# A decoder trunk with 32 experts: expert weights in 2048-column pieces, both turns in one place, and a written order of ScalarE and VectorE at the end

## The chip, the cores and the metric

The kernel runs on one core of one Trainium2 chip. The metric is device microseconds (us) from the first to the last instruction of one execution with what lies around it; lower is better. TensorE is PE here (its weight loads are PEld), VectorE is DVE, ScalarE is ACT, GpSimd is POOL, SyncE is SP. All data are fp32.

## The reference

One decoder layer over 1024 tokens of width 1024, then a final RMSNorm. The first half of the layer mixes tokens (an SSD group, a forgetting-attention group, a convolution group, one output projection); the second is a mixture of 32 gated-MLP experts, two for each token:

```
x = x + g_m * hybrid_mixer(rms_norm(x, norm_mix_g) * (1.0 + sc_m) + sh_m, ...)
h = rms_norm(x, norm_ffn_g) * (1.0 + sc_f) + sh_f
# per token: one group of 8 experts, in it the two best, with weights sw
hid = silu(xb @ w_gate[e]) * (xb @ w_up[e])      # 1024 -> 512
y   = hid @ w_down[e]                            # 512 -> 1024
out = zeros.at[stok].add(ys[dest] * sw)          # the two shares of a token
x = x + g_f * out
return rms_norm(x, final_norm_g)
```

## The kernel before

**An fp32 product.** TensorE multiplies a rounded form of fp32, so each operand is cut in two: `hi` is a cast of it (made by ACT), `lo` is what the cast left (a subtraction by DVE). A product is three matmuls: hi with `xh`, hi with `xl`, lo with `xh`, where `xh` and `xl` are the two parts of the tokens. So every weight that arrives from DRAM passes once through ACT (`phi`) and once through DVE (`plo`) before PE may use it.

**The experts.** From about 645 us to 1237 us the program goes through the experts in order. An expert has 6 MB of weights: gate (G), up (U) and down (D), each 2 tiles of 2048 columns ("halves"), loaded by SP into a ring of 18 such halves (`NHALF`, `load_half`) that runs ahead of the use. `piece` (L1325 to L1329) takes 1024 columns: one cast and one subtraction, with three buffers for each result. 6 matmuls use a piece, so an expert is 12 pieces and 72 matmuls of 512 columns. The loop body of expert e runs G(e), U(e), then D(e-1), so the hidden activations `hid` have time to be made. Two "turns" (groups of 128x128 transposes on PE with a split by ACT and DVE behind them) feed this: `xpose(e+1)` turns the 128 gathered tokens of the next expert (8 transposes `ps_xg`, then `xh`, `xl`), and `turn_hidden` turns `hid` (4 transposes `ps_ht`, then `hh`, `hl`). In before, `turn_hidden(e-1)` is called ahead of the second piece of G(e) (`before_down`), `xpose` ahead of the second piece of D(e-1). When D(e-1) is done, DVE scales it by the router's weight and the gate `gf` (two `early` operations, L1374), and POOL adds it into the result in DRAM with an indirect DMA, called the scatter here (L1378); POOL also gathers the next tokens (L1308).

**Order of the work.** Each engine runs its own list in order. A scheduler makes the lists from the order of the code and from its estimates; instructions that are pinned (`pin`) keep the order in which the code writes them.

**Ahead of the experts.** `row_spread(gf, ...)` (L1282) spreads a row over all partitions by 8 pairs of small matmuls and two copies. In the mixer, the q and k tiles (`qk_tile`, matmuls `ps_pr`) run on PE while DVE does the convolution (`cy`); one transpose, `ps_nc` (L487), takes a running sum `ncu` (L481) that DVE makes.

**The end.** When the last but one share has been scattered, SP loads the eight blocks of the result (`x_d`); blocks 0 to 5 are normed and written at once, without the share of expert 31 (ACT: `Square` with a sum; DVE and POOL: the factor; DVE: the product). The rows among them that have such a share are gathered into `xr` (the tile `xg`) by POOL. Blocks 6 and 7 get the share of expert 31 by matmuls with a matrix of places (`ps_ad`), `xr` gets it by an addition; `xr` is normed too, and POOL scatters it over the output last (L1485).

## Time and profile before

| | |
|---|---|
| three runs, median | 1276.93 us (1276.75 to 1277.41) |
| the profiled execution | 1275.77 us, of which the span of its instructions 1273.9 us |
| PE busy | 1186.6 us, 93% of the span |
| DVE, ACT, POOL busy | 980.5, 736.4, 268.2 us |
| mean granted TensorE clock | 0.972 |
| one steady expert | 18.46 us (scatters at 904.48 and 922.97 us, for one pair) |

Times inside the trace count from the first instruction. "Busy" is an engine's time in instructions; where rows carry a bracket, it is how long the engine stood idle ahead of that row, and what ended the wait. Rows that the profile puts together as "x3" overlap: their time is from the start of the first to the end of the last.

### The profile page before, as it was taken

To read this page: it belongs to the slowest core of one execution; us is meant where nothing else is said; L and a number is where in the kernel's file an instruction comes from. 1 tells how busy PE (TensorE), PEld (TensorE's weight loads), DVE (VectorE), ACT (ScalarE), POOL (GpSimd) and SP (SyncE) were. 2 spreads that over 40 slices of the span, in tenths; PEclk is the share of its full clock that TensorE was granted. 3 is DMA by queue.
4 is the path that set the end of the run, shared out by engine and by line. 5 is a ranking of instruction groups with operands and counts; after the bars stand their busy time and mean duration, and the time that the engine had idled before them with its cause. 6 is when DMAs were issued, how large, how long until landed. Compare 5 with 4: busy or idle time off the path is not lost. (4 is left out here: it accounts for less than half of the span.)

```text
span 1273.9 us, 17238 instructions
## 1 busy us (share of the span) xinstructions
PE 1186.6 (93%) x6079; PEld 928.3 (73%) x6079; DVE 980.5 (77%) x1395; ACT 736.4 (58%) x1145; POOL 268.2 (21%) x200
## 2 busy tenths in 40 slices
PE   6999989999999779999779999999999999999993
PEld 4676757868678568778568877777877787787772
DVE  4789992145265676575559999999999999999985
ACT  4323322343354656563258877777877787777763
POOL 3110313100100353432111221122112212211112
PEclk9999999999999989999879999999999999999997
DMA  9316667633201553734889999999999999999726
GB/s 361 140 42 220 210 196 224 160 108 89 78 17 59 148 155 100 262 98 183 304 305 343 361 356 372 366 354 367 369 359 372 356 358 387 363 381 366 236 53 257
DMA packets 93339, 313.21 MB, mean 246 GB/s; under 512 B 23894, under 2 KB 34310, under 8 KB 70976
## 3 DMA queue, kind: packets, MB, share of 16 engines
q1 hardware_dynamic: 60750, 256.25, 54.8%
q10 hardware_dynamic: 14242, 32.51, 7.4%
q0 software_dynamic: 18256, 23.30, 7.2%
q8 instruction: 49, 0.80, 0.3%
q14 instruction: 42, 0.34, 0.1%
HBM read 289.22 MB, written 39.88 MB: 258 GB/s over the span
## 5 line engine op out<-in xcount | busy, mean ns | idle before, releaser
L1342 PE MATMUL ps_gu<-plo,xh 128*128 128x512 f32 x512 | 209.1, 408 | 9.1 <-DVE plo L1328 9.0
L1340 PE MATMUL ps_gu<-phi,xh 128*128 128x512 f32 x512 | 203.3, 397 | 1.4 <-ACT xh L127 1.4
L1328 DVE TENSOR_TENSOR plo<-wx,phi 128x1024 fp32r<-128x1024 f32 x166 | 198.1, 1220 | 7.8 <-ACT phi L1328 5.5
L1328 ACT CAST phi<-wx 128x1024 fp32r<-128x1024 f32 x166 | 173.1, 1054 | 50.7 <-PE ps_gu L1341 40.8
L1341 PE MATMUL ps_gu<-phi,xl 128*128 128x512 f32 x512 | 200.8, 392 | 0.0
L1378 POOL DMA_INDIRECT x_d<-early,toki x31 | 74.9, 2416 | 400.7 <-DVE early L1374 386.0
L1328 ACT CAST phi<-w 128x1024 fp32r<-128x1024 f32 x110 | 115.3, 1050 | 60.4 <-PE ps_gu L1341 53.1
L1328 DVE TENSOR_TENSOR plo<-w,phi 128x1024 fp32r<-128x1024 f32 x110 | 130.7, 1220 | 7.2 <-ACT phi L1328 6.3
L1342 PEld LDWEIGHTS ps_gu<-plo,xh 128*128 128x128 f32 x512 | 96.3, 188 | 40.2 <-DVE plo L1328 20.8
L1340 PEld LDWEIGHTS ps_gu<-phi,xh 128*128 128x128 f32 x512 | 96.5, 189 | 20.2 <-ACT xh L127 1.8
L1341 PEld LDWEIGHTS ps_gu<-phi,xl 128*128 128x128 f32 x512 | 96.5, 188 | 19.6
L1368 PE MATMUL ps_d<-phi,hh 128*128 128x512 f32 x256 | 100.4, 393 | 0.7 <-ACT hh L127 0.7
L1369 PE MATMUL ps_d<-phi,hl 128*128 128x512 f32 x256 | 100.5, 393 | 0.0
L1370 PE MATMUL ps_d<-plo,hh 128*128 128x512 f32 x256 | 96.4, 393 | 0.0
L182 PE MATMUL ps_pr<-h_hi,whi 128*128 128x512 f32 x224 | 91.5, 409 | 0.0
L184 PE MATMUL ps_pr<-h_hi,wlo 128*128 128x512 f32 x224 | 88.8, 396 | 1.3 <-POOL wlo L128 1.3
L183 PE MATMUL ps_pr<-h_lo,whi 128*128 128x512 f32 x224 | 89.2, 398 | 0.0
L225 DVE SCALAR_TENSOR_TENSOR cy<-u_t,cmw,cy 128x1024 f32<-128x1024 f32 x60 | 86.4, 1440 | 2.3 <-ACT cy L222 1.4
L128 POOL TENSOR_TENSOR wlo<-wraw,whi 128x1024 fp32r<-128x1024 f32 x14 | 40.0, 2866 | 161.1 <-ACT whi L127 142.9
L1328 DVE TENSOR_TENSOR plo<-cy,phi 128x1024 fp32r<-128x1024 f32 x44 | 53.8, 1222 | 6.0 <-ACT phi L1328 5.2
L994 PE MATMUL ps_wo<-wo_hi,yh 128*128 128x512 f32 x128 | 55.1, 431 | 2.1 <-ACT yh L127 2.1
L1368 PEld LDWEIGHTS ps_d<-phi,hh 128*128 128x128 f32 x256 | 48.3, 189 | 10.9 <-ACT hh L127 0.9
(405 smaller groups left out, 2570.9 us busy)
## 6 DMA issues: line engine op xcount, KB each, us to landing
w<-in_w_gu_dram SPq DMA_DIRECT2D x54, 1024.0 KB
wx<-in_w_gu_dram SPq DMA_DIRECT2D x50, 1024.0 KB
...
```

What stands on the lines that cost most here:

```text
L182: PE.matmul(ps, hi[:, kt, :], h_hi[hf][:, kt, :], start=(kt == 0), stop=False)
L183: PE.matmul(ps, hi[:, kt, :], h_lo[hf][:, kt, :], start=False, stop=False)
L184: PE.matmul(ps, lo[:, kt, :], h_hi[hf][:, kt, :], start=False, stop=(kt == KT - 1))
L225: yield lambda t=t, k=k: V.scalar_tensor_tensor(cy[:, :, t], v128(u_t[:, t, k:k + T]), cmw[:, t, k:k + 1], cy[:, :, t], op0=ALU.mult, op1= ...
L1328: last[:] = [S.copy(hi, raw).ins, V.tensor_tensor(lo, raw, hi.bitcast(F32), op=ALU.subtract).ins]
L1340: PE.matmul(ps, xh[:, kt], hi[:, ks], start=(kt == 0), stop=False)
L1341: PE.matmul(ps, xl[:, kt], hi[:, ks], start=False, stop=False)
L1342: PE.matmul(ps, xh[:, kt], lo[:, ks], start=False, stop=(kt == KT - 1))
L1368: PE.matmul(pd[n], hh[:, f], hi[:, ns], start=(f == 0), stop=False)
L1369: PE.matmul(pd[n], hl[:, f], hi[:, ns], start=False, stop=False)
L1370: PE.matmul(pd[n], hh[:, f], lo[:, ns], start=False, stop=(f == 3))
L1378: G.indirect_dma_start(x1_d[:, :], bass.IndirectOffsetOnAxis(ap=toki[:, e:e + 1], axis=0), yo[:, :], None, bounds_check=T - 1, oob_is_err= ...
```

## The change

1. **Pieces of 2048 columns.** `piece` becomes `pieces`: one cast and one subtraction of 2048 columns for a half, two buffers for each result in place of three. PE's order in a piece is 8 matmuls with hi, then 4 with lo, pinned. Halves that lie in two tiles (`wy`) and the last down projection stay in two parts of 1024.
2. **Turns together.** `xpose(e+1)` and `turn_hidden(e)` are both called in the middle of D(e-1). `hh` and `hl` lie in one tile `hx`.
3. **Room.** The ring has 17 halves; `w2` goes.
4. **The last experts.** D(30) is placed ahead of G(31), and its share has a buffer of its own (`free[1]`), not `early`. Its weights are loaded ahead of those of G(31).
5. **Rows.** `row_spread(gf)` moves from before expert 0 into the middle of the body of expert 1, `row_spread(fng)` into that of expert 30.
6. **`ps_nc`** moves behind the second q and k tile (t == 1) and is pinned.
7. **The end.** The order of ACT and DVE is written out: squares of the six blocks on ACT, four products on DVE ahead of the scaling of the last share, the addition to `xr` on DVE (in before POOL), the addition of EPS on POOL, output in halves of a block.

```diff
-NHALF = 18
+NHALF = 17
...
-DC, NC_ = 2, 15
+DC, NC_ = 2, 14
...
-        if t == 0:
+        if t == 1:
             pc = bank("ps_nc")
-            PE.transpose(pc[:32, 0:P], ncu.rearrange("p h b -> p (h b)"), ident)
+            pin(PE.transpose(pc[:32, 0:P], ncu.rearrange("p h b -> p (h b)"), ident))
...
-        order += [(e, 0), (e, 1), (e - 1, 2)] if e < NE - 1 else [(e, 0), (e - 1, 2), (e, 1)]
+        order += [(e, 0), (e, 1), (e - 1, 2)] if e < NE - 1 else [(e - 1, 2), (e, 0), (e, 1)]
...
-            room(ew.tile([P, 2048], F32, name="w2"))
...
-    row_spread(gf, sl[0:8, :])
...
+        def pieces(e, m, s):
+            a, b, both = wts[e, m][s]
+            hi = ex.tile([P, 2048], F32R, tag="phi", name="phi", bufs=2)
+            lo = ex.tile([P, 2048], F32R, tag="plo", name="plo", bufs=2)
+            if both is None or (e, m) == (NE - 1, 2):
+                parts = ((a, slice(0, 1024)), (b, slice(1024, 2048)))
+            else:
+                parts = ((both, slice(0, 2048)),)
+            for raw, cs in parts:
+                last[:] = [S.copy(hi[:, cs], raw).ins, V.tensor_tensor(lo[:, cs], raw, hi[:, cs].bitcast(F32), op=ALU.subtract).ins]
+            return [(hi[:, cs], lo[:, cs], (cs.stop - cs.start) // 512) for _, cs in parts]
...
+                for hi, lo, n in pieces(e, m, s):
+                    for k in range(n):
+                        ks = slice(512 * k, 512 * (k + 1))
+                        pin(PE.matmul(ps, xh[:, k0 + k], hi[:, ks], start=(k0 + k == 0), stop=False))
+                        pin(PE.matmul(ps, xl[:, k0 + k], hi[:, ks], start=False, stop=False))
+                    for k in range(n):
+                        ks = slice(512 * k, 512 * (k + 1))
+                        pin(PE.matmul(ps, xh[:, k0 + k], lo[:, ks], start=False, stop=(k0 + k == KT - 1)))
+                    k0 += n
...
+            def middle():
+                next_tokens(e + 1)
+                turns()
+                if e == 1:
+                    row_spread(gf, sl[0:8, :])
+                if e == NE - 2:
+                    row_spread(fng, early[0:8, D:D + P])
...
+            if e == NE - 1:
                 down(e - 1, *hts[e - 1])
                 load_next()
-                hid = hidden(pg, gate_or_up(e, 1, xh, xl))
+            pg = gate_or_up(e, 0, xh, xl, turns if e == 1 else None)
+            load_next()
+            hid = hidden(pg, gate_or_up(e, 1, xh, xl))
+            load_next()
+            if e == 0:
+                next_tokens(1)
+            elif e < NE - 1:
+                down(e - 1, *hts[e - 1], middle)
                 load_next()
...
+        sqs = [square(xbs[b]) for b in range(FB)]
+        for b in range(4):
+            finish(b, sqs[b])
         for n in range(2):
             ns = slice(512 * n, 512 * (n + 1))
-            split(yh[:, ns], yl[:, ns], yo_l[:, ns])
+            pin(V.scalar_tensor_tensor(yo_l[:, ns], pd[n], wtab[:, NE - 1:NE], gf[:, ns], op0=ALU.mult, op1=ALU.mult))
...
+            pin(S.copy(yh[:, ns], yo_l[:, ns]))
+            pin(V.tensor_tensor(yl[:, ns], yo_l[:, ns], yh[:, ns].bitcast(F32), op=ALU.subtract))
+        pin(V.tensor_tensor(xr, xr, yo_l, op=ALU.add))
+        sx = square(xr)
+        for b in range(4, FB):
+            finish(b, sqs[b])
```

**VectorE, one steady expert.** Before, from the `hid` of one expert to the first subtractions of the next body (`plo` are the subtractions, `xl` and `hl` the splits of the two turns):

```order
L1348 TENSOR_TENSOR hid<-hid,ps_gu 128x512
L1328 TENSOR_TENSOR plo<-wx,phi 128x1024
L128 TENSOR_TENSOR xl<-ps_xg,xh 128x512 x2
L1328 TENSOR_TENSOR plo<-wx,phi 128x1024 x2
L1374 SCALAR_TENSOR_TENSOR early<-ps_d_6666,wtab,gf 128x512
L1374 SCALAR_TENSOR_TENSOR early<-ps_d_6667,wtab,gf 128x512
L1328 TENSOR_TENSOR plo<-wx,phi 128x1024
L128 TENSOR_TENSOR hl<-ps_ht,hh 128x512
L1328 TENSOR_TENSOR plo<-wy,phi 128x1024 x2
L1328 TENSOR_TENSOR plo<-w_4443,phi 128x1024 x4
L1328 TENSOR_TENSOR plo<-xq_3956,phi 128x1024 x2
```

In the changed kernel, the same stretch of the same expert:

```order
L1331 TENSOR_TENSOR plo<-wx,phi 128x2048 x2
L126 TENSOR_TENSOR xl<-ps_xg,xh 128x512 x2
L126 TENSOR_TENSOR hx<-ps_ht,hx 128x512
L1391 SCALAR_TENSOR_TENSOR early<-ps_d_7683,wtab,gf 128x512
L1391 SCALAR_TENSOR_TENSOR early<-ps_d_7684,wtab,gf 128x512
L1331 TENSOR_TENSOR plo<-wx,phi 128x2048
L1331 TENSOR_TENSOR plo<-wy,phi 128x1024 x2
L1331 TENSOR_TENSOR plo<-w_4443,phi 128x2048 x2
L1355 TENSOR_TENSOR hid<-hid,ps_gu 128x512
L1331 TENSOR_TENSOR plo<-xq_3956,phi 128x2048
```

Between the subtraction of the first gate half and that of the second there now stand five operations in a row (`xl` twice, `hx`, `early` twice); before, they were spread between five subtractions.

**TensorE around `ps_nc`.** Before, it stands within the matmuls of a q or k tile, ahead of `ps_arr` and `ps_a` (products for the modulation):

```order
L182 MATMUL ps_pr_1408<-h_hi_106,whi 128x512
L183 MATMUL ps_pr_1408<-h_lo_108,whi 128x512
L487 MATMUL ps_nc<-ident,ncu 32x128
L423 MATMUL ps_arr<-aacc,ind_r 128x512 x2
L415 MATMUL ps_a_1367<-at,cond_119 32x512 x8
L184 MATMUL ps_pr_1408<-h_hi_106,wlo 128x512
L182 MATMUL ps_pr_1408<-h_hi_106,whi 128x512
```

Now `ps_arr` and a first group of `ps_a` stand alone there:

```order
L181 MATMUL ps_pr_1314<-h_lo_109,whi 128x512
L182 MATMUL ps_pr_1314<-h_hi_107,wlo 128x512
L421 MATMUL ps_arr<-aacc,ind_r 128x512 x2
L413 MATMUL ps_a_1362<-at,cond_119 32x512 x8
L180 MATMUL ps_pr_1403<-h_hi_106,whi 128x512
L181 MATMUL ps_pr_1403<-h_lo_108,whi 128x512
```

and `ps_nc` comes after 48 further matmuls `ps_pr`, behind the second tile:

```order
L181 MATMUL ps_pr_1428<-h_lo_109,whi 128x512
L182 MATMUL ps_pr_1428<-h_hi_107,wlo 128x512
L485 MATMUL ps_nc<-ident,ncu 32x128
L421 MATMUL ps_arr<-aacc,ind_r 128x512 x2
L413 MATMUL ps_a_1481<-at,cond_119 32x512 x8
L180 MATMUL ps_pr_1522<-h_hi_106,whi 128x512
```

**VectorE at the end.** Before, from the split of the last `hid` on (L1293 is the addition of EPS, L1296 the product of a block, L1374 the scaling of the last share, `yo_l` its split):

```order
L128 TENSOR_TENSOR hl<-ps_ht,hh 128x512
L1328 TENSOR_TENSOR plo<-wx,phi 128x1024
L1293 TENSOR_SCALAR s_11117<-s_11117 128x1
L1296 SCALAR_TENSOR_TENSOR wx<-wx,s_11117 128x1024
L1374 SCALAR_TENSOR_TENSOR wx<-ps_d_11073,wtab,gf 128x512
L1374 SCALAR_TENSOR_TENSOR wx<-ps_d_11074,wtab,gf 128x512
L1293 TENSOR_SCALAR s_11123<-s_11123 128x1
L1293 TENSOR_SCALAR s_11129<-s_11129 128x1
L1296 SCALAR_TENSOR_TENSOR wx<-wx,s_11123 128x1024
L1296 SCALAR_TENSOR_TENSOR wy<-wy,s_11129,wx 128x1024
L1293 TENSOR_SCALAR s_11135<-s_11135 128x1
L128 TENSOR_TENSOR yo_l<-wx,yo_h 128x512
```

Now (L1486 is the product of a block, L1494 the scaling, L1501 the addition to `xr`):

```order
L126 TENSOR_TENSOR hx<-ps_ht,hx 128x512
L1486 SCALAR_TENSOR_TENSOR wx<-wx,s_10363,wy 128x1024
L1486 SCALAR_TENSOR_TENSOR wx<-wx,s_10367,wy 128x1024
L1486 SCALAR_TENSOR_TENSOR wx<-wx,s_10371,wy 128x1024
L1486 SCALAR_TENSOR_TENSOR wx<-wx,s_10375,wy 128x1024
L1494 SCALAR_TENSOR_TENSOR cy<-ps_d_10325,wtab,gf 128x512
L1494 SCALAR_TENSOR_TENSOR cy<-ps_d_10326,wtab,gf 128x512
L1500 TENSOR_TENSOR yo_l<-cy,yo_h 128x512 x2
L1501 TENSOR_TENSOR xg<-xg,cy 128x1024
L1486 SCALAR_TENSOR_TENSOR wx<-wx,s_10379,wy 128x1024
L1486 SCALAR_TENSOR_TENSOR wx<-wx,s_10383,wy 128x1024
L1522 SCALAR_TENSOR_TENSOR s_10412<-s_10412 128x1
```

The additions of EPS are gone from DVE, four products come first, and the scaling, the split and the addition follow one another.

## Rows read from the trace of the kernel before

**Rows 1.** The page: GB/s moved by DMA in 40 equal slices of the span.
```profile
GB/s 361 140 42 220 210 196 224 160 108 89 78 17 59 148 155 100 262 98 183 304 305 343 361 356 372 366 354 367 369 359 372 356 358 387 363 381 366 236 53 257
```

**Rows 2.** Windows: busy us of PE, PEld, DVE, ACT, POOL; clock, DMA share, GB/s.
```profile
300.00:400.00 100.00, 99.82 (x563) 72.86 (x562) 48.61 (x122) 42.81 (x81) 8.95 (x7) 1.00 0.18 56
...
800.00:900.00 100.00, 98.32 (x456) 79.67 (x455) 96.17 (x98) 78.13 (x90) 17.29 (x10) 1.00 0.99 363
```

**Rows 3.** Waits from 700 to 1200: total us, times, longest us.
```profile
PEld ps_gu L1342 <- DVE plo L1328: 18.7, 25, 0.8
...
SPq L1198 <- DVE plo L1328: 208.1, 107, 4.4
```

**Rows 4.** Timeline of PE in one steady expert: start us, us.
```profile
913.20 0.39 PE L1340 MATMUL ps_gu<-phi,xh 128*128 128x512 f32 x1
...
914.56 0.39 PE L1340 MATMUL ps_gu<-phi,xh 128*128 128x512 f32 x1
...
923.02 1.03 PE L1318 MATMUL ps_xg<-ident,xg 128*128 128x128 f32 x8
...
925.86 0.50 PE L1342 MATMUL ps_gu<-plo,xh 128*128 128x512 f32 x1 [0.33 <-DVE plo L1328]
```

**Rows 5.** Timeline of DVE in the same expert.
```profile
917.81 1.28 DVE L128 TENSOR_TENSOR xl<-ps_xg,xh 128x512 fp32r<-128x512 f32 x2
...
919.01 2.35 DVE L1328 TENSOR_TENSOR plo<-wx,phi 128x1024 fp32r<-128x1024 f32 x2
...
921.28 1.41 DVE L1374 SCALAR_TENSOR_TENSOR early<-ps_d,wtab,gf 128x512 f32<-128x512 f32 x2
```

**Rows 6.** Timeline of ACT in the same expert.
```profile
916.17 1.06 ACT L127 CAST xh<-ps_xg 128x512 fp32r<-128x512 f32 x2
...
917.12 2.01 ACT L1328 CAST phi<-wx 128x1024 fp32r<-128x1024 f32 x2
```

**Rows 7.** Timeline of POOL: the first and the thirtieth scatter, of 30.
```profile
684.70 3.47 POOL L1378 DMA_INDIRECT x_d<-early,toki  x1 [4.21 <-DVE early L1374]
...
1218.51 2.28 POOL L1378 DMA_INDIRECT x_d<-early,toki  x1 [16.15 <-DVE early L1374]
```

**Rows 8.** Timeline of PE around the transpose ps_nc, in the front.
```profile
169.72 0.40 PE L183 MATMUL ps_pr<-h_lo,whi 128*128 128x512 f32 x1
...
175.38 0.37 PE L487 MATMUL ps_nc<-ident,ncu 128*32 128x128 f32 x1 [5.27 <-DVE ncu L481]
...
176.54 2.94 PE L415 MATMUL ps_a<-at,cond 128*32 128x512 f32 x16
```

**Rows 9.** Timeline of DVE there.
```profile
175.06 0.18 DVE L481 TENSOR_SCALAR ncu<-early 128x32 f32<-128x32 f32 x1
```

**Rows 10.** Timeline of PE ahead of expert 0.
```profile
643.86 3.75 PE L1282 MATMUL ps_row<-sl,ident 8*128 8x128 f32 x16 [5.48 <-DMA sl<-g_rows]
...
647.54 1.97 PE L1318 MATMUL ps_xg<-ident,xg 128*128 128x128 f32 x8
```

**Rows 11.** Timeline of DVE there: the largest of seven overflow operations.
```profile
648.17 0.39 DVE L1394 TENSOR_TENSOR c<-cnt,j 128x224 f32<-128x224 f32 x1
```

**Rows 12.** Timelines of POOL, SP, ACT and DVE at the end.
```profile
1231.90 2.29 POOL L1378 DMA_INDIRECT x_d<-early,toki  x1 [11.11 <-DVE early L1374]
...
1238.75 0.81 SPq L1446 DMA_DIRECT2D wx<-x_d  x2
...
1251.93 1.06 ACT L1292 ACTIVATE wx<-w 128x1024 f32<-128x1024 f32 x1 [2.01 <-DMA w<-x_d]
...
1246.44 1.43 DVE L1374 SCALAR_TENSOR_TENSOR wx<-ps_d,wtab,gf 128x512 f32<-128x512 f32 x2 [0.17 <-PE ps_d L1370]
...
1256.60 3.36 DVE L1296 SCALAR_TENSOR_TENSOR w<-w,s,wx 128x1024 f32<-128x1024 f32 x1 [0.66 <-POOL s L1294]
...
1264.20 1.28 DVE L1296 SCALAR_TENSOR_TENSOR xg<-xg,s,wx 128x1024 f32<-128x1024 f32 x1 [0.73 <-POOL s L1294]
...
1265.77 1.06 POOL L1485 DMA_INDIRECT out_dram<-xg,toki  x1 [1.61 <-DVEq L1489]
```

More of the change, by code (lines that the diff above doesn't have):

```diff
@@ L49 @@
 ZW = 2
-QT = 1
 DEPTH = 5
@@ L1194, in load_half @@
             src = (w_gu[e, m_] if m_ < 2 else w_dn[e]).rearrange("p a c -> p (a c)")[:, 2048 * (i % 2):2048 * (i % 2 + 1)]
-            w, both = halves[i % NHALF][0:2], halves[i % NHALF][2]
-            pieces = ((both, src),) if both is not None and i < 6 * NE - 6 else zip(w, (src[:, 0:1024], src[:, 1024:2048]))
+            w = halves[i % NHALF]
+            both = w[2]
+            pieces = ((both, src),) if both is not None and i < 6 * NE - 6 else zip(w[0:2], (src[:, 0:1024], src[:, 1024:2048]))
             for dst, sc_ in pieces:
@@ L1361, in down @@
             pd = [bank("ps_d0", "pj"), bank("ps_d1", "pj")]
-            for f in range(4):
-                if f == QD and then:
+            f0 = 0
+            for s in range(2):
+                if s and then:
                     then()
-                hi, lo = piece(e, 2, f)
-                for n in range(2):
-                    ns = slice(512 * n, 512 * (n + 1))
-                    PE.matmul(pd[n], hh[:, f], hi[:, ns], start=(f == 0), stop=False)
-                    PE.matmul(pd[n], hl[:, f], hi[:, ns], start=False, stop=False)
-                    PE.matmul(pd[n], hh[:, f], lo[:, ns], start=False, stop=(f == 3))
-            yo = yo_l if e == NE - 1 else early[:, 0:D]
+                for hi, lo, w in pieces(e, 2, s):
+                    fn = [(f0 + i // 2, i % 2, slice(512 * i, 512 * (i + 1))) for i in range(w)]
+                    for f, n, ns in fn:
+                        pin(PE.matmul(pd[n], hh[:, f], hi[:, ns], start=(f == 0), stop=False))
+                        pin(PE.matmul(pd[n], hl[:, f], hi[:, ns], start=False, stop=False))
+                    for f, n, ns in fn:
+                        pin(PE.matmul(pd[n], hh[:, f], lo[:, ns], start=False, stop=(f == 3)))
+                    f0 += w // 2
+            if e == NE - 1:
+                return pd
+            yo = free[1] if e == NE - 2 else early[:, 0:D]
             for n in range(2):
@@ L1436, in mixer_moe @@
                 overflow()
-            if e == NE - 2:
-                free = [h for k in (8, 7, 6) for w in wts[order[3 * NE - k]] for h in w]
         yo_l, junk, tok = free[0:3]
@@ L1453, in mixer_moe, with square, finish @@
         V.tensor_scalar(place, tok[:, 0:T - nf], tok_l[:, 0:1], None, op0=ALU.is_equal)
[L1454 to L1459 removed]
+        pd = down(NE - 1, *turn_hidden(NE - 1, hid))
+        def square(src):
+            s3 = late.tile([P, 2], F32, tag="s3e", name="s3", bufs=7)
+            pin(S.activation(junk, src, AF.Square, scale=1.0 / 32, accum_out=s3[:, 0:1]))
+            G.tensor_scalar(s3[:, 0:1], s3[:, 0:1], EPS, None, op0=ALU.add)
+            G.tensor_tensor(s3[:, 1:2], s3[:, 0:1], half[:, 0:1], op=ALU.pow)
+            return s3
+        def finish(b, s3):
+            pin(V.scalar_tensor_tensor(xbs[b], xbs[b], s3[:, 1:2], fng, op0=ALU.mult, op1=ALU.mult))
+            nc.sync.dma_start(out[b * P:(b + 1) * P, :], xbs[b])
+        sqs = [square(xbs[b]) for b in range(FB)]
+        for b in range(4):
+            finish(b, sqs[b])
         for n in range(2):
             ns = slice(512 * n, 512 * (n + 1))
[L1462 removed]
+            pin(V.scalar_tensor_tensor(yo_l[:, ns], pd[n], wtab[:, NE - 1:NE], gf[:, ns], op0=ALU.mult, op1=ALU.mult))
+        yh = ex.tile([P, 2048], F32R, tag="phi", name="yo_h", bufs=2)[:, 0:D]
+        yl = ex.tile([P, 2048], F32R, tag="plo", name="yo_l", bufs=2)[:, 0:D]
+        for n in range(2):
+            ns = slice(512 * n, 512 * (n + 1))
+            pin(S.copy(yh[:, ns], yo_l[:, ns]))
[4 more added lines that the diff above has]
+            finish(b, sqs[b])
+        s3s, psss = [], []
         for b in range(FB, NB):
@@ L1465, in mixer_moe @@
             pss = []
+            s3s.append(s3)
+            psss.append(pss)
             for n in range(2):
```

95 lines of the change are left out of this document (36 added, 59 removed).

## The prediction

> **What bounds the kernel now.** I read the windows first. In the experts PE is busy for 98.3 of 100 us at clock 1.00, DVE for 96.2, ACT for 78.1, and DMA for 99% of the time at 363 GB/s [rows 2]. Three resources are near full, so I looked for which wait ends last. The waits say so for PE: between 700 and 1200 us its weight loads for the lo matmuls wait 25 times, 18.7 us in total, for the subtraction on DVE [rows 3]; that is once for each of the 27 experts in that stretch, all but two. SP's loads wait 107 times, 208 us, for the same subtractions, which empty the ring [rows 3]; they run ahead of the use, so DMA is not what PE waits for.
>
> One expert takes (1218.51 - 684.70)/29 = 18.41 us [rows 7]. Its matmuls come every (914.56 - 913.20)/6 = 0.227 us [rows 4], so 72 of them are 16.32 us. The 8 transposes of `ps_xg` take about 1.0 [rows 4], the 4 of `ps_ht` half of that by number. That makes 17.8; the other 0.6 is the stall on DVE and the slower start behind it (0.33 of it is seen as idle time) [rows 4]. So the change can win at most about 0.6 us x 29 = 17 us in this stage.
>
> **Pieces of 2048 columns.** The price of a 2048-column operation is in no row, so I bound it. DVE: two subtractions of 1024 together take 2.35 us, two of 512 take 1.28 [rows 5]; one alone is what is left of the pair when one spacing is taken off, so the spacings are about 1.13 and 0.60, a slope of 0.53 for 512 columns. Then 2048 columns take 1.13 + 2 x 0.53 = 2.19 (estimate). From above, two operations alone would be 2 x 1.22 = 2.44; from below, twice the slope of the rows, 2.12. I take 2.19. ACT: two casts of 1024 take 2.01, two of 512 take 1.06 [rows 6], spacings 0.96 and 0.48: no saving is seen, so 2048 takes 1.92 (bounds 1.9 and 2.1). Per expert DVE gets rid of 6 x (2 x 1.13 - 2.19) = 0.4 us of its work. That alone would end most of the 0.6 us stall.
>
> But the new order makes a longer chain. With two buffers, the cast of the next expert's first gate half waits until the hi matmuls of the first half of D are done. From there, engine by engine: hand-off from PE 0.2 (a matmul lasts 0.39 and the next issues after 0.227 [rows 4]); cast 1.92; subtraction 2.19; then, on DVE in this order, `xl` twice 1.2, `hx` 0.6, `early` twice 1.33 (1.41 less what overlaps) [rows 5]; subtraction of the second gate half 2.19; hand-off and slower start of PE 0.25; then 4 + 12 + 12 + 8 = 36 matmuls until the hi matmuls of the next D are done, 8.16. The sum is 18.04; three hand-offs between ACT and DVE of about 0.05 make it 18.2. This closes a loop, so it is the period as long as it is longer than PE's own 17.8. So I expect **18.2 us in place of 18.41, 29 times: -6 us**. PE would still stall once for each expert, now at the lo matmuls of the second gate half.
>
> The Trainium skill says, in "Vector Engine (DVE) Microarchitecture Reference", section "Measured stream behaviour on trn2", that ScalarE takes 0.833 ns per column and about 98 ns more per instruction. By that a cast of 2048 would take 1.80 us and the loop 18.1, another -3 us in all; rows 6 show no such fixed part between 512 and 1024 columns (though the 512-column casts read another memory), so I keep 1.92.
>
> **Turns together** change where the transposes stand, not their number: nothing on PE but one restart less (about 0.1), which is in the sum above. **The ring of 17** gives up 1 of 18 halves of run-ahead. DMA moves 363 GB/s x 18.41 us = 6.7 MB for each expert now; at 18.2 us that is 367 GB/s, and slices show 381 and 387 [rows 1]. A ring of 17 halves is nearly three experts deep, some 50 us of work at six halves an expert; the stage is to become 6 us shorter, which this covers. I cost the ring at nothing; without the cover DMA at 363 GB/s would hold the period at 18.41 and take the 6 us back.
>
> **`ps_nc`.** PE stands idle 5.27 us at 175.38 until `ncu` is made on DVE at 175.06 [rows 8, 9], and the products `ps_a` behind it run at half clock: 16 in 2.94 us [rows 8]. Now `ps_arr`, `ps_a` and 48 matmuls `ps_pr` (48 x 0.23 = 11 us) stand ahead of it, so the wait ends while PE works. PE is busy for 99.8 of 100 us from 300 on [rows 2], so what is won here is mostly carried on. **-5 us** (bounds 0, if a later stage waits for something that does not move, and -6.3 with the clock).
>
> **Rows and the start of the experts.** Before, PE waits 5.48 us for a row to land, spreads it at 643.86 (3.75 us), and turns the tokens at 647.54 [rows 10]. Now the turn comes first: at the earliest at 643.9, at the latest at 647.5; I take 645.5, when it is still slow from the idle time, -2. The spread costs PE about 1.9 in expert 1, half of the 3.75 that it took at half clock. The overflow operations, idle-time work of DVE so far, come between subtractions in expert 2 (seven, the largest 0.39 [rows 11]): +1.5. In sum **+1 us** (-2 to +3).
>
> **The end.** Before, the last share is scaled at 1246.44, `xr` is finished at 1265.48 and scattered at 1265.77, and the span ends 8.1 us later [rows 12]. On the way lie three things: ACT waits for a block until 1251.93, one product takes 3.36 us in place of 1.28 (POOL adds into `xr` beside it), and `xr` comes after all the others [rows 12]. Now D(30) stands 24 matmuls (5.4 us) earlier, so the loads start at about 1233.3 in place of 1238.75. From the scaling on the chain is: scaling 1.4, cast and split of the second half 1.2, addition 1.2, square 1.25, factor 1.0, product 1.2, together 7.3, and the squares of blocks 6 and 7 between (4 x 0.7, by the 512-column cast [rows 6]) delay POOL's part by about 1.5: scatter 9 us behind the scaling, not 19.3. **-10 us** (-5, if the blocks land late again, to -11). ACT's list has the square of block 0 ahead of `hx` of expert 31: if the block came after 1238.9, D(31) would wait for it; the 5.4 us cover that.
>
> **Sum.** -6 - 5 + 1 - 10 = -20 us. The profiled execution took 1275.77 (span 1273.9), so 1255.8; the median of the runs lies 1.2 above the profiled one: **1257**.
>
> **Rivals.**
> 1. *The long operations don't pay (slower).* A subtraction of 2048 takes 2.44 and a cast 2.1, and the subtraction can't begin before the whole cast is done. The loop holds two subtractions and a cast: 18.2 + 0.5 + 0.2 = 18.9, in place of 18.41: +14 us, against -14 for the rest. So from a subtraction of about 2.45 on, the kernel is not faster, and at 2.55 (19.1) it is 5 us slower, 1282. For it: DVE is at 96% and the two buffers let nothing run ahead; against it: the spacings of rows 5. The Trainium skill has the rule, in "Perfetto Trace Analysis", section "Optimizing Scalar/DVE Operations": engines that are not saturated but cause bubbles elsewhere should have their instructions broken up, saturated ones grouped. ACT is the one (78%), DVE the other (96%) [rows 2], so the rule speaks both for and against.
> 2. *The stall goes altogether.* The period falls to PE's own 17.8: -17 in the stage, 1246.
> 3. *The front's gain is lost later* (a wait for POOL or for a load between 400 and 640): 1262.
> 4. *DMA caps the experts.* Its share is 0.99 already [rows 2]. If 363 GB/s were all, the loads would fall back by 0.2 us an expert, 6 us of the run-ahead in all: 1257 again, and only if the run-ahead were near nothing now, 1263.
>
> **How the numbers follow.** The forecast 0.55 (by itself 1250 to 1263), rival 2 0.13, rival 3 0.12, between forecast and break-even (period 18.4 to 18.9, or rival 4 at its worst: 1263 to 1275) 0.09, rival 1 beyond that 0.11. Range 1245 to 1272: it leaves out rival 1 and little of the others. A measurement can tell 0.2%, 2.6 us. Faster 0.86, same 0.04, slower 0.10.
>
> **What would show it.** Right: subtractions of 2048 at 2.2 spaced; scatters 18.2 apart; one wait of PE for DVE for each expert at the second gate half; no idle time at `ps_nc`; POOL's last scatter about 9 us behind the scaling. Wrong: PE waiting for casts (ACT), scatters over 18.4 apart, SP's loads landing just ahead of their use, or ACT idle at the square of block 0 with `hx` behind it.

## The result and the profile after

The change makes the kernel faster: the median of four runs is 1263.26 us (1261.77 to 1265.88) against 1276.84 us of four runs of the kernel before, a ratio of 0.9896 (95%: 0.9882 to 0.9911), so -13.6 us of the -20 that the sum had. The profiled execution is the slowest of the four, 1265.88 us with a span of 1264.1; a second profile of the same kernel (experiment 12 below) has a span of 1260.4. I use both and say which.

**The experts.** Windows of the kernel after; columns as in [rows 2].

```profile
300.00:400.00 100.00, 99.83 (x567) 73.49 (x566) 48.62 (x122) 43.15 (x82) 8.92 (x7) 1.00 0.18 56
800.00:900.00 100.00, 99.65 (x468) 81.16 (x467) 94.17 (x72) 74.17 (x59) 31.98 (x11) 1.00 0.98 371
```

PE went from 98.3 to 99.7 of 100 us, DVE from 96.2 to 94.2. The waits between 700 and 1200 us (total us, times, longest), to hold against [rows 3]; the first line is of the kernel before:

```profile
ACT phi L1328 <- PE ps_gu L1341: 100.7, 178, 1.0
...
ACT phi L1331 <- PE ps_gu L1345: 75.0, 96, 1.5
...
PEld ps_gu L1348 <- DVE plo L1331: 11.7, 26, 0.5
```

The wait of PE for DVE is still there once for each expert, 0.45 us instead of 0.75. ACT waits for PE to give a buffer back, 0.8 us each time; it did so before too, 178 times and 0.57 us each, so this wait alone does not show the predicted loop. The links of the loop can be read off the timelines of ACT, DVE and PE in one steady expert:

```profile
911.34 1.91 ACT L1331 CAST phi<-cy 128x2048 fp32r<-128x2048 f32 x1 [0.86 <-PE ps_d L1381]
913.15 1.07 ACT L125 CAST xh<-ps_xg 128x512 fp32r<-128x512 f32 x2
...
913.28 2.29 DVE L1331 TENSOR_TENSOR plo<-cy,phi 128x2048 fp32r<-128x2048 f32 x1
915.50 1.28 DVE L126 TENSOR_TENSOR xl<-ps_xg,xh 128x512 fp32r<-128x512 f32 x2
916.69 0.68 DVE L126 TENSOR_TENSOR hx<-ps_ht,hx 128x512 fp32r<-128x512 f32 x1
917.29 1.40 DVE L1391 SCALAR_TENSOR_TENSOR early<-ps_d,wtab,gf 128x512 f32<-128x512 f32 x2
918.61 4.48 DVE L1331 TENSOR_TENSOR plo<-w,phi 128x2048 fp32r<-128x2048 f32 x2
...
920.50 0.39 PE L1345 MATMUL ps_gu<-phi,xl 128*128 128x512 f32 x1
920.94 1.20 PE L1348 MATMUL ps_gu<-plo,xh 128*128 128x512 f32 x4
```

From the start of one row to the next: cast 1.94, subtraction 2.22, `xl` 1.19, `hx` 0.60, `early` 1.32; the pair of subtractions takes 4.48, of which the first is 2.2. So the lo part of the second gate half is ready at about 920.8; the matmul ahead was issued at 920.50 and the next could have gone at 920.73, but goes at 920.94. From the cast on, DVE has no gap up to there. The stall is short, and it comes in nearly every round (26 times for 27 experts).

**The front.** Timeline of PE, against [rows 8]: `ps_nc` no longer waits, and `ps_a` runs at full clock (16 in 1.92 us, before 2.94).

```profile
168.25 1.92 PE L413 MATMUL ps_a<-at,cond 128*32 128x512 f32 x16
...
181.37 0.27 PE L485 MATMUL ps_nc<-ident,ncu 128*32 128x128 f32 x1
```

**The spreads and the start.** Timeline of PE, against [rows 10]; the second group is the spread of `fng` in the body of expert 30.

```profile
640.27 1.94 PE L1315 MATMUL ps_xg<-ident,xg 128*128 128x128 f32 x8 [5.25 <-DMA xg<-h_d,toki]
642.03 0.79 PE L1344 MATMUL ps_gu<-phi,xh 128*128 128x512 f32 x1
...
1203.45 1.15 PE L1280 MATMUL ps_row<-early,ident 8*128 8x128 f32 x8
1205.28 1.15 PE L1280 MATMUL ps_row<-early,ident 8*128 8x128 f32 x8 [0.68 <-ACT wy L1281]
1206.37 0.80 PE L1380 MATMUL ps_d<-phi,hx 128*128 128x512 f32 x1
1206.96 0.63 PE L1381 MATMUL ps_d<-phi,hx 128*128 128x512 f32 x1
1207.39 0.63 PE L1380 MATMUL ps_d<-phi,hx 128*128 128x512 f32 x1
```

The experts start at 642.0; before, `ps_xg` alone started at 647.54. But the spread, now inside an expert, costs more than its matmuls: from 1203.45 to 1206.37 are 2.9 us with a wait for ACT in it, and the matmuls behind it come every 0.43 us in place of 0.227, the spacing of the lower clock: the granted clock is 0.64 from 1206.3 to 1211.0 and 1.00 in the window from 800 to 900. The same happens behind the spread of `gf` at 673.77 (0.61 from 676.6 to 681.0).

**The end.** Timelines of POOL (the scatters of experts 29 and 30 and the one over the output), SP, ACT, PE and DVE, against [rows 12]:

```profile
1212.46 3.35 POOL L1393 DMA_INDIRECT x_d<-early,toki  x1 [18.33 <-DVE early L1391]
1220.97 3.43 POOL L1393 DMA_INDIRECT x_d<-cy,toki  x1 [5.16 <-DVE plo L1331]
...
1254.93 1.07 POOL L1538 DMA_INDIRECT out_dram<-xg,toki  x1 [0.48 <-DVE wx L1528]
...
1228.84 3.78 SPq L1466 DMA_DIRECT2D wx<-x_d  x8
...
1232.26 1.06 ACT L1480 ACTIVATE cy<-wx 128x1024 f32<-128x1024 f32 x1 [3.83 <-DMA wx<-x_d]
1233.31 0.56 ACT L125 CAST hx<-ps_ht 128x512 fp32r<-128x512 f32 x1
...
1243.00 1.06 ACT L1480 ACTIVATE cy<-wx 128x1024 f32<-128x1024 f32 x1 [4.18 <-DMA wx<-x_d]
...
1245.33 1.12 ACT L1499 CAST yo_h<-cy 128x512 fp32r<-128x512 f32 x2
...
1228.15 0.66 PE L1361 MATMUL ps_ht<-ident,hid 128*128 128x128 f32 x4 [0.85 <-DVE hid L1355]
1233.93 0.80 PE L1380 MATMUL ps_d<-phi,hx 128*128 128x512 f32 x1 [5.12 <-ACT hx L125]
...
1245.98 0.50 PE L1516 MATMUL ps_ad<-yo_h,place 128*128 128x512 f32 x1 [3.74 <-ACT yo_h L1499]
...
1241.86 1.40 DVE L1494 SCALAR_TENSOR_TENSOR cy<-ps_d,wtab,gf 128x512 f32<-128x512 f32 x2
```

Two waits that before did not have stand here. ACT waits for block 0 with `hx` behind it in its list, so PE stands idle 5.12 us ahead of D(31); and ACT waits for block 4 with `yo_h` behind it. The cast `yo_h` starts 3.5 us behind the scaling of the share (1241.86), which is most of the 3.74 us that PE stands idle ahead of its product. The chain of work that ended last (start, us, what) goes through those loads in one step:

```profile
918.69 2.21 DVE plo L1331
...
1232.17 12.01 DMA wx<-x_d
```

### The profile page after: what moved, and what is told of

It is laid out like the page before. It is cut to its first block, busy times and chain, and to the rows that moved or that the text cites. A ratio compares the mean times of both kernels' runs of the same rounds, so it can differ in the third digit from the quotient of the medians.

```text
span 1264.1 us, 16568 instructions
## 1 busy us (share of the span) xinstructions
PE 1188.4 (94%) x6079; PEld 932.0 (74%) x6079; DVE 959.4 (76%) x1221; ACT 710.0 (56%) x977; POOL 338.5 (27%) x206
## 4 chain that ended last, share of the span: by engine, by line
PE 74%; DVE 8%; DMA 7%; issue 4%; ACT 3%; POOL 2%; SPq 1%; POOLq 0%; DVEq 0%; ACTq 0%
PE ps_gu L1348 8%; PE ps_gu L1345 7%; PE ps_gu L1344 7%; PE ps_d L1380 4%; PE ps_d L1381 4%; PE ps_d L1383 4%; PE ps_pr L180 4%; DVE plo L1331 4%; PE ps_pr L181 4%; PE ps_pr L182 4%; PE ps_o L599 2%; PE ps_xg L1315 2%; PE ps_wo L992 2%; PE ps_wo L993 2%; PE ps_wo L994 2%
## 5 line engine op out<-in xcount | busy, mean ns | idle before, releaser
L1331 DVE TENSOR_TENSOR plo<-wx,phi 128x2048 fp32r<-128x2048 f32 x88 | 199.7, 2290 | 15.2 <-ACT phi L1331 15.1
L1331 ACT CAST phi<-wx 128x2048 fp32r<-128x2048 f32 x88 | 168.0, 1909 | 71.9 <-PE ps_gu L1345 39.8
L1348 PE MATMUL ps_gu<-plo,xh 128*128 128x512 f32 x512 | 143.0, 397 | 1.5
L1348 PEld LDWEIGHTS ps_gu<-plo,xh 128*128 128x128 f32 x512 | 94.6, 189 | 30.2 <-DVE plo L1331 11.7
L1331 DVE TENSOR_TENSOR plo<-w,phi 128x2048 fp32r<-128x2048 f32 (+1 forms) x48 | 107.3, 2245 | 12.1 <-ACT phi L1331 12.0
L1331 ACT CAST phi<-w 128x2048 fp32r<-128x2048 f32 (+1 forms) x48 | 89.6, 1872 | 43.5 <-PE ps_gu L1345 23.0
L1380 PE MATMUL ps_d<-phi,hx 128*128 128x512 f32 x256 | 105.8, 413 | 5.1 <-ACT hx L125 5.1
L1381 PE MATMUL ps_d<-phi,hx 128*128 128x512 f32 x256 | 102.7, 401 | 0.0
L1305 POOL DMA_INDIRECT xq<-h_d,toki x16 | 41.8, 2614 | 143.7 <-PE ps_xg L1315 125.1
L1305 POOL DMA_INDIRECT xg<-h_d,toki x16 | 38.6, 2415 | 151.8 <-PE ps_xg L1315 103.7
L1383 PE MATMUL ps_d<-plo,hx 128*128 128x512 f32 x256 | 71.9, 397 | 0.0
L1380 PEld LDWEIGHTS ps_d<-phi,hx 128*128 128x128 f32 x256 | 49.3, 193 | 15.5 <-ACT hx L125 5.4
## 6 DMA issues: line engine op xcount, KB each, us to landing
wy<-in_w_gu_dram SPq DMA_DIRECT2D x30, 512.0 KB, 10.2
```

What stands on the lines that cost most here:

```text
L1331: last[:] = [S.copy(hi[:, cs], raw).ins, V.tensor_tensor(lo[:, cs], raw, hi[:, cs].bitcast(F32), op=ALU.subtract).ins]
L1348: pin(PE.matmul(ps, xh[:, k0 + k], lo[:, ks], start=False, stop=(k0 + k == KT - 1)))
L1380: pin(PE.matmul(pd[n], hh[:, f], hi[:, ns], start=(f == 0), stop=False))
L1381: pin(PE.matmul(pd[n], hl[:, f], hi[:, ns], start=False, stop=False))
L1383: pin(PE.matmul(pd[n], hh[:, f], lo[:, ns], start=False, stop=(f == 3)))
```

## The experiments

All in one table. "first" is the start of the scatter of expert 0; "29" the time from it to the scatter of expert 29; "period" the mean from the third to the twenty-seventh scatter; "30" from the scatter of expert 29 to that of 30; "end" from there to the end of the span. These five are of the one profiled execution, in us; median, lowest and highest time, and the ratio to the kernel before with its 95% interval, are of all runs. (The pair of scatters named for the kernel before, at 904.48 and 922.97, lies 18.49 apart, not 18.46.) "first" does not measure an edit that leaves the front alone: in the eleven profiles with the changed front it lies between 679.6 and 686.5, and their first gate matmul between 640.1 and 644.9. No run bears the number 7.

| kernel | first | 29 | period | 30 | end | median (range) | ratio |
|---|---|---|---|---|---|---|---|
| before | 684.7 | 533.8 | 18.45 | 13.4 | 42.0 | 1276.84 | |
| after | 682.9 | 529.6 | 18.12 | 8.5 | 43.1 | 1263.26 (1261.8–1265.9) | 0.9896 (0.9882–0.9911) |
| 12 after, again | 681.1 | 529.7 | 18.12 | 8.4 | 41.2 | 1264.45 (1262.2–1266.8) | 0.9904 (0.9880–0.9929) |
| 1 `ps_nc` back | 689.5 | 530.0 | 18.12 | 8.7 | 43.4 | 1269.64 (1265.3–1273.4) | 0.9934 (0.9911–0.9957) |
| 2 parts of 1024 | 681.6 | 519.1 | 17.76 | 7.8 | 41.5 | 1253.58 (1251.8–1256.4) | 0.9827 (0.9807–0.9848) |
| 3 turns apart | 683.2 | 529.5 | 18.21 | 12.1 | 43.1 | 1268.04 (1265.9–1269.7) | 0.9928 (0.9908–0.9947) |
| 9 1024, turns apart | 680.2 | 517.9 | 17.79 | 10.5 | 43.1 | 1251.09 (1250.2–1253.6) | 0.9789 (0.9759–0.9819) |
| 11 1024, three buffers | 684.6 | 519.2 | 17.76 | 10.2 | 43.0 | 1254.28 (1251.1–1259.1) | 0.9811 (0.9787–0.9834) |
| 10 before, four buffers | 683.7 | 513.6 | 17.72 | 15.0 | 44.9 | 1257.94 (1256.9–1259.0) | 0.9845 (0.9825–0.9864) |
| 6 `early` later | 686.5 | 521.5 | 17.88 | 10.0 | 41.6 | 1264.15 (1261.4–1267.7) | 0.9903 (0.9870–0.9936) |
| 5 spread ahead of D | 681.6 | 528.6 | 18.12 | 8.9 | 42.2 | 1264.68 (1259.6–1267.1) | 0.9895 (0.9854–0.9936) |
| 4 other order at the end | 684.1 | 529.6 | 18.12 | 8.5 | 41.4 | 1265.02 (1263.7–1268.9) | 0.9915 (0.9889–0.9941) |
| 13 half the loads | 681.2 | 529.4 | 18.12 | 8.9 | 41.0 | 1263.89 (1262.3–1265.2) | 0.9898 (0.9876–0.9919) |
| 8 1024, spread and end moved | 679.6 | 518.8 | 17.76 | 9.8 | 42.0 | 1253.19 (1251.5–1257.8) | 0.9819 (0.9782–0.9855) |

The theory to start with was that of the prediction: a loop through the 2048-column cast and subtraction sets the period, `ps_nc` gives 5 us, and the end lost its gain to ACT's order. The rivals are named with each run.

**1. `ps_nc` where it was**, all else as changed.

```diff
-        if t == 1:
+        if t == 0:
...
-            pin(PE.transpose(pc[:32, 0:P], ncu.rearrange("p h b -> p (h b)"), ident))
+            PE.transpose(pc[:32, 0:P], ncu.rearrange("p h b -> p (h b)"), ident)
```

> The changed kernel with the transpose ps_nc put back into the first q and k tile, unpinned, as before. My theory: the wait for ncu and the half-clock products behind it return, 5.3 + 1.0 us, and the rest of the program carries the shift: about 5 to 6 us slower than the changed kernel, near 1269, with PE idle about 5 us at ps_nc. Rival: the later chain (POOL and loads between 400 and 640 us) absorbs it: no more than 1.5 us slower.

The wait is back. PE and DVE:

```profile
176.31 0.37 PE L485 MATMUL ps_nc<-ident,ncu 128*32 128x128 f32 x1 [5.24 <-DVE ncu L479]
...
175.99 0.18 DVE L479 TENSOR_SCALAR ncu<-early 128x32 f32<-128x32 f32 x1
```

The first scatter comes 6.6 us later than in after, the median 5.2 us above that of the second set of after, 6.4 above the first. The first gate matmul stands at 648.45, outside the 640.1 to 644.9 of the others. What was won at 175 us is not lost later: the term of -5 is borne out, rival 3 is out.

**2. Every half in two parts of 1024**, in the same two buffers of 2048, which hold four parts. PE then takes 4 matmuls with hi and 2 with lo in turn, where it took 8 and 4.

```diff
-            if both is None or (e, m) == (NE - 1, 2):
+            if True:
                 parts = ((a, slice(0, 1024)), (b, slice(1024, 2048)))
```

> The changed kernel with every half cast and subtracted in two operations of 1024 columns (same buffers, same loads, same place of the turns; PE takes 4 hi matmuls, then 2 lo ones). Theory A (DVE's amount of work sets the pace: the larger operations save its fixed parts): six more subtractions and casts an expert, about 0.07 us each, so a period back at 18.4 to 18.5 us and the kernel 8 to 10 us slower. Theory B (my loop, cast then subtraction, of the forecast sets it): the subtraction can start after half the cast, the loop gets 0.8 us shorter, the period falls to PE's own 17.8 to 17.9 and the kernel is 6 to 8 us faster than the changed one.

The same window as above in this kernel:

```profile
800.00:900.00 100.00, 100.00 (x478) 83.28 (x476) 98.42 (x103) 78.84 (x91) 23.74 (x12) 1.00 1.00 374
```

PE is busy all the time, no wait for `plo` is left, and the period is 17.76 us: that is PE's own work. DVE is busier than before the change (98.4) and no longer stalls anyone. So long operations save DVE work and cost PE time. That a subtraction of 2048 cannot begin before the whole cast is done, and the matmuls not before the whole subtraction, would explain it; this run also changes PE's order of hi and lo, and only experiment 6 takes the two apart, in part. The price is 0.36 us for each expert, 10.5 us in the stage and about 10 us in the median.

**3. The turn of `hid` back in the gate**, pieces of 2048 kept.

```diff
-                turns()
...
+                turns()
                 down(e - 1, *hts[e - 1])
...
-            pg = gate_or_up(e, 0, xh, xl, turns if e == 1 else None)
+            pg = gate_or_up(e, 0, xh, xl, turns if 1 <= e < NE - 1 else None)
```

> The changed kernel with the turn of the hidden activations back in the gate of the next expert (ahead of its second half), so only the place of the four transposes and of hx changes. By my loop hx (0.6 us on DVE) leaves the stretch between the subtractions of the two gate halves but comes back behind the second: period 18.1 to 18.2, the same time within 2 us. Rival: turns together are what shortened the period, since PE restarts less and DVE is not interrupted in the gate: period 18.4, 7 us slower.

The stall moves, it does not go. Waits, 700 to 1200:

```profile
PEld ps_gu L1345 <- DVE xl L126: 14.9, 24, 1.1
```

The period is 18.21, 0.09 more; most of the 3.6 to 4.8 us in the median lies behind the scatter of expert 29 (12.1 in place of 8.4), where the turn now stands ahead of D(30).

**9, 11, 10. What takes the stall away?** Experiment 9 has the edits of 2 and 3 together. Experiment 11 has pieces of 1024 in three buffers of their own, as before the change, but keeps PE's order (hi first, then lo) and the turns in one place. Experiment 10 is the program before with a fourth buffer, for which the ring gives up one half (and `w2` and one buffer of `NC_`, as in the change):

```diff
-NHALF = 18
+NHALF = 17
...
-            hi = ex.tile([P, 1024], F32R, tag="phi", name="phi", bufs=3)
-            lo = ex.tile([P, 1024], F32R, tag="plo", name="plo", bufs=3)
+            hi = ex.tile([P, 1024], F32R, tag="phi", name="phi", bufs=4)
+            lo = ex.tile([P, 1024], F32R, tag="plo", name="plo", bufs=4)
```

> Operations of 1024 columns and the turn of the hidden activations back in the gate: the steady order of the kernel before, but with the pinned order of PE and room for four pieces and not three. Theory A (the place of the turns is what the change won): the stall of before returns, period 18.3 to 18.45, about 1262. Theory B (the fourth piece of room, or PE's order, is what removed the stall): period 17.8, 1254.

> The changed kernel with pieces of 1024 columns in three buffers of their own, as before the change, but with the changed place of the turns and the pinned order of PE (4 hi matmuls, 2 lo). The opposite cell of the same question: theory A (room): a stall returns, period 18.2 to 18.5, 1264 to 1270. Theory B (order): 17.8, 1252 to 1255.

> The kernel before with one thing more: four buffers of 1024 columns for each of the two results (three before), paid with one half of the ring (17). Nothing else of the change. Theory A (the room for a fourth piece removes the stall: cast and subtraction run one piece further ahead): period 17.8 to 17.9 and 25 waits gone, 14 to 17 us faster than before, about 1260 to 1263. Theory B (PE's pinned order, hi first and lo last, gives the subtraction its time): the period stays at 18.4 and the time within 3 us of before.

All three run at PE's own pace (17.79, 17.76, 17.72). Window of experiment 10:

```profile
800.00:900.00 100.00, 100.00 (x478) 83.16 (x477) 99.03 (x104) 81.69 (x91) 32.94 (x12) 1.00 1.00 369
```

Experiment 11 shows that three buffers are enough with the new order of PE (with the turns together), and experiment 10 that the pinned order of hi and lo is not needed with four. But experiment 10 is not the kernel before with one thing more. PE's list in before is not pinned, and the scheduler made another one for this program: the 8 transposes `ps_xg`, which before stand among the matmuls of the gate (923.02 in [rows 4]), stand where the code has them, behind the sixth matmul of D:

```profile
907.20 0.39 PE L1369 MATMUL ps_d<-plo,hh 128*128 128x512 f32 x1
907.43 1.03 PE L1317 MATMUL ps_xg<-ident,xq 128*128 128x128 f32 x8
```

They stand in D in every kernel without the stall (2, 8, 9, 10, 11), and all of these have the ring of 17. So neither theory is shown: the stall of before may have gone by the room, by the place of these transposes (ahead of matmuls that still hold a buffer, they may delay its giving back) or by both. Four buffers with the old list of PE, three buffers with the transposes in D and nothing pinned, and a ring of 17 alone were not run. Experiment 10, with what the scheduler made of it, gives -19.3 us, more than the whole change. Experiment 9 has the lowest median of the study, 1251.09 us, 12 us below the changed kernel; against experiments 2 and 8 its 2 us lie within the spread of the runs.

**6. `early` behind the second subtraction**, with pieces of 2048. This takes 1.3 us out of the loop and leaves all work in.

```diff
+                if s and m == 0:
+                    pin(last[1])
+                    flush()
...
+            if 0 < e < NE - 3:
+                pend.append(share)
```

> The changed kernel (pieces of 2048) with DVE's two scalings of a share (early, 1.33 us) placed behind the subtraction of the second gate half and no longer ahead of it, for experts 1 to 28. Theory: these are part of the loop (cast, subtraction, xl, hx, early, subtraction) that sets the period of 18.12; without them the loop is 16.8 and the period falls to what PE needs, 17.76 to 17.85: 8 to 10 us faster than the changed kernel, 1253 to 1256, and the 26 waits for plo are gone. Rival: what shortened the period with pieces of 1024 is PE's finer order of hi and lo or the earlier release of buffers: the period stays at 18.0 or above.

The wait shrinks from 26 times, 11.7 us, to

```profile
PEld ps_gu L1356 <- DVE plo L1335: 2.1, 4, 0.5
```

and the period falls by 0.24 to 17.88: the loop is the right picture, since an operation of DVE that feeds nothing of PE's shortened it by its place alone. This is 0.24 of the 0.36 us that pieces of 1024 bring, with the long pieces and PE's order 8 and 4 kept. The stage is 8.1 us shorter, but the median is that of after. In the profiled execution the first scatter is 3.7 to 5.5 us later than in the two of after and "30" is 1.5 longer. Some 3 us of the former are the edit's own: its pin holds the second gate half of expert 1 too, where the turn of `hid` stands ahead. There DVE waits for `hx` with the subtraction behind it, and PE for the subtraction:

```profile
663.90 0.69 DVE L126 TENSOR_TENSOR hx<-ps_ht,hx 128x512 fp32r<-128x512 f32 x1 [4.95 <-ACT hx L125]
...
666.85 1.20 PE L1356 MATMUL ps_gu<-plo,xh 128*128 128x512 f32 x4 [1.78 <-DVE plo L1335]
```

From the first gate matmul to the first scatter it takes 43.9 us, 40.8 and 41.0 in the two profiles of after. The rest is the front's own variation and the 1.5 in "30", which stays open.

**5. The spreads between U and D**, their matmuls pinned together.

```diff
...
+                if e == 1:
+                    row_spread(gf, sl[0:8, :])
+                if e == NE - 2:
+                    row_spread(fng, early[0:8, D:D + P])
                 down(e - 1, *hts[e - 1], middle)
```

> The changed kernel with both row spreads pinned between U and D of the same loop bodies, not in the middle of D with the 12 transposes. The two loop bodies that hold a spread now take about 4 and 3.6 us more than their neighbours. Theory: of that about 1.7 each is the half clock of TensorE that follows 28 small matmuls in a row with a wait among them; apart from the transposes the spread costs only its own 2.9 us, so 2 to 3.5 us are won in all, 1260 to 1261, and the matmuls behind the spread run 0.227 us apart. Rival: the spread alone (16 small matmuls and the wait for a copy) is enough for the clock to fall: no gain within 1 us, and half clock behind it as now.

Mixed. PE at expert 1 and at expert 30:

```profile
669.84 2.04 PE L1280 MATMUL ps_row<-sl,ident 8*128 8x128 f32 x16
...
672.38 0.39 PE L1380 MATMUL ps_d<-phi,hx 128*128 128x512 f32 x1
...
1197.18 2.05 PE L1280 MATMUL ps_row<-early,ident 8*128 8x128 f32 x16
...
1200.25 0.63 PE L1381 MATMUL ps_d<-phi,hx 128*128 128x512 f32 x1
```

The wait for ACT is gone, and at expert 1 the matmuls behind run at full clock (granted 1.00 from 672 to 676). At expert 30 the same 16 matmuls are followed by the lower clock (0.70 from 1200 to 1205), and the interval there stays 21.6 us. Nothing shows in the median, so this is no way to the missing time.

**4 and 13. The end.** Experiment 4 puts `hx` ahead of the squares on ACT, and `yo_h` ahead of those of blocks 4 and 5:

```diff
-        sqs = [square(xbs[b]) for b in range(FB)]
-        for b in range(4):
+        with tc.issue_after(turned[0].ins):
+            sqs = [square(xbs[b]) for b in range(4)]
+        for b in range(2):
...
         sx = square(xr)
+        sqs += [square(xbs[b]) for b in range(4, FB)]
```

> The changed kernel with another written order at the end: ACT's hx of expert 31 ahead of the square of block 0, the casts of the last share ahead of the squares of blocks 4 and 5, DVE's products of blocks 2 and 3 behind the scaling of the last share. Theory: the 5.1 us that D(31) waited for hx, and ACT's 4 us in front of the casts, were the order's own, not the loads': D(31) starts 5 us earlier, and the end comes 4 to 7 us earlier, 1256 to 1259. Rival: the loads of the eight blocks, which end about 1243, set the end whatever the order: less than 1.5 us gained.

ACT and POOL:

```profile
1230.06 0.59 ACT L1368 CAST hx<-ps_ht 128x512 fp32r<-128x512 f32 x1 [0.42 <-PE ps_ht L1361]
...
1240.14 1.28 ACT L1501 CAST yo_h<-cy 128x512 fp32r<-128x512 f32 x2
...
1245.74 1.06 ACT L1481 ACTIVATE cy<-wx 128x1024 f32<-128x1024 f32 x1
...
1244.61 1.14 POOL L1482 TENSOR_SCALAR s<-s 128x1 f32<-128x1 f32 x1 [3.47 <-ACT cy L1481]
...
1254.37 1.08 POOL L1541 DMA_INDIRECT out_dram<-xg,toki  x1 [0.48 <-DVE wx L1531]
```

D(31) no longer waits, `yo_h` starts 17.9 us behind the scatter of expert 30 (22.4 in experiment 12), and yet the last scatter follows that of expert 30 by 32.2 us (31.9 in experiment 12). The time is the rival's, the reason only in part: the chain that ended last goes through the loads up to the square of block 3 at 1239.0, but from 1240.3 on no engine waits for a load in this profile. The 4.4 us that `yo_h` won are lost in the order behind it. The squares of blocks 4 and 5 that were put back now stand ahead of those of `ps_ad`, and the chain runs from 1244.6 to 1252.4 over POOL's small operations on the factors, with DVE's products of blocks 4 and 5 ahead of that of `xr`. Experiment 13 goes at the other wait: of each of the eight blocks only the left half is loaded, so its output is not the result.

```diff
-            nc.sync.dma_start(xbs[b], x1_d[b * P:(b + 1) * P, :])
+            nc.sync.dma_start(xbs[b][:, 0:512], x1_d[b * P:(b + 1) * P, 0:512])
```

> The changed kernel with only the left half of each of the eight blocks loaded at the end (2 MB, not 4; the right half of the output is left undefined). Theory: the end is bound by these loads, the last of which lands 14 us after its issue: the squares of the last blocks start about 6 us earlier, and POOL's last scatter and the end come 4 to 6 us earlier. Rival: D(31) and the work behind it on ACT and DVE set the end: less than 2 us.

ACT and PE:

```profile
1237.83 1.06 ACT L1480 ACTIVATE cy<-wx 128x1024 f32<-128x1024 f32 x1 [2.12 <-DMA wx<-x_d]
...
1232.35 0.80 PE L1380 MATMUL ps_d<-phi,hx 128*128 128x512 f32 x1 [5.42 <-ACT hx L125]
```

The square of block 4 starts 18.3 us behind the scatter of expert 30 (22.0 and 20.1 in the two profiles of after), and the end is the same (41.0): D(31) still stands behind block 0. So two chains of nearly equal length seem to end here: load, squares, factors; and block 0, `hx`, D(31), the share. To shorten one shows the other, though in experiment 4 the new order has also made the first one longer behind the loads. Both together, with nothing else changed, was not tried.

**8. Pieces of 1024, the spreads of 5, the end of 4 with the blocks loaded in the order 0 to 7** and the square of `xr` behind those of blocks 4 and 5.

```diff
-LORD = (0, 1, 2, 3, 6, 7, 4, 5)
+LORD = (0, 1, 2, 3, 4, 5, 6, 7)
```

> Three edits at once: operations of 1024 columns in the changed kernel, the row spreads between U and D, and another end (hx of expert 31 ahead of the squares, blocks loaded in order 0 to 7, casts of the last share ahead of squares 4 and 5, square of xr behind them, products 2 and 3 behind the scaling). Theory: against the run with 1024 columns alone (1253.6) the spreads give 2 to 3 us and the end 4 to 7, since POOL's last scatter waits for the writes of blocks 0 to 5, which now are loaded first: 1244 to 1248. Rival: the end is bound by the loads of the eight blocks, and only the spreads pay: 1250 to 1252.

No gain over experiment 2: blocks 6 and 7 come last now, and PE stands idle ahead of `ps_ad`, which needs them, until about 14 us behind the start of the loads at 1216.65. That it waits for them is inferred; the view names no releaser:

```profile
1230.53 2.05 PE L1518 MATMUL ps_ad<-wx,ident 128*128 128x512 f32 x2 [8.98 <-issue]
```

**12. The changed kernel once more**, beside the others, for a second profile.

> The changed kernel unaltered, for comparison on the same chip: 1261 to 1266 expected, steady period 18.12.

It has the same period and the same kinds of wait as the first, its first scatter is 1.8 us earlier, and D(31) waits 3.0 us instead of 5.1.

## Why the prediction was right, and where it was not

Direction and range were right, the size was 6 us too large. By stage, from before to experiment 12 (1262.2 us): up to the first scatter -3.6, 29 intervals -4.1, scatter 30 -5.0, end -0.8; in sum -13.5. (The slower profile of after: -1.8, -4.2, -4.9, +1.1; -9.8.) The account of the loop and of `ps_nc` held. That of the end did not, and a forecast within its range does not bear it out.

- **Period.** Forecast 18.2, measured 18.12. Each term of the loop was met within 0.03 us (cast 1.94 for 1.92, subtraction 2.2 for 2.19, `xl` 1.19 for 1.2, `hx` 0.60 for 0.6, `early` 1.32 for 1.33), and experiment 6 shows that it is a loop. What the prediction did not ask is whether the same order with pieces of 1024 would have no loop at all: experiment 2 says so. The Trainium skill's figure for ScalarE ("Vector Engine (DVE) Microarchitecture Reference", section "Measured stream behaviour on trn2") gave an estimate of 1.80 for the cast. The trace agrees with it for the distance from one start on ACT to the next, 1.81; the row's duration is 1.91, and the subtraction in the loop starts 1.94 behind the cast. So the loop of 18.1 by the Trainium skill's figure came closer by luck: what the sum had too long were the three hand-offs of 0.05 (from the cast to the end of the second subtraction the trace has 9.47 us, the sum 9.58 with them). The Trainium skill says in "Perfetto Trace Analysis", section "Optimizing Scalar/DVE Operations", that grouping can improve throughput where the engine is saturated. Here grouping took DVE from 98.4 to 94.2 of 100 us and still cost the kernel 10 us, against the ungrouped form (experiment 2).
- **The stage.** -6 was forecast and -4.1 measured (experiment 12), in other parts: the first three intervals are 1.8 longer, the next 25 together 8.9 shorter, and the one ahead of the scatter of expert 29 is 3.0 longer (21.5), for the spread of `fng` in it. In before that spread lay between the scatters of experts 29 and 30; the prediction put it in no stage.
- **`ps_nc`.** -5, measured 5 to 6 by experiment 1.
- **Rows and start.** The turn came at its early bound: 640.3, which is 643.9 less the 3.4 by which PE is ahead there (at 632.66, before 636.02). The first gate matmul is 7.9 us earlier than before (9.8 in experiment 12), 3.4 of it by the front and 4.5 by the row, where the sum had 2. But at the first scatter only 1.8 to 3.6 are left. The spread was put at 1.9; it takes 2.9, for a wait for ACT between its halves, and the lower clock behind it takes 1.7 more (12 matmuls in 4.4 us, at full clock 2.7). The net (-1.8 and -3.6 where -5 + 1 was forecast) came out near by luck, from two terms that were both too small.
- **The end: the step that failed.** -10 was forecast from the scaling of the last share on: POOL's last scatter 9 us behind it in place of 19.3. It came 13.1 us behind it (12.1 in experiment 12), which is -6 to -7. The missing 3 to 4 us are for the most part `yo_h`, which stands in ACT's list behind the squares of blocks 4 and 5, and these wait for their loads; it starts 3.5 us (2.5) behind the scaling. And the scaling itself came later: 29.4 us (28.2) behind the scatter of expert 29, before 27.9, although the spread of `fng` no longer lies between. So by scatters it is -5.0 from that of expert 29 to that of 30, and -0.8 from there to the end of the span. The sum said of block 0 and `hx`: "the 5.4 us cover that". They did not. The share of expert 30 was ready 5.5 us behind the scatter of expert 29 (before 13.1), at 1218.0, but its scatter started only at 1220.97, and the loads, which hang on it, were issued 7.9 us behind that (before 6.9). So they came at 1228.84, 0.7 us behind the transposes of the last `hid` (1228.15), much as before (1238.75 and 1238.18), and of the 5.4 us nothing was left; in experiment 12 they came 1.4 us ahead of the transposes, and D(31) waited 3.0 in place of 5.1. With block 0 ahead of it, `hx` waited, as the last of the signs of "wrong" had it. That the scatter of expert 30 waits for that of expert 29 to land would fit (both add into the same tensor in DRAM), but no run here separates it. And the second chain, that of the loads, has nearly the same length: in experiments 4 and 13 each remedy alone gives nothing.
- **Rivals.** 1 is out as priced (the subtraction takes 2.2, not 2.45), but its direction is that of experiment 2: the long operations don't pay. 2 came true only with pieces of 1024, and nearly with experiment 6 (17.88). 3 is out by experiment 1. 4 is out: the same load runs at 374 GB/s in experiment 2.
